# Gates and branch projections of the two mixers with the roles of weights and activations exchanged

## The chip, the cores and the metric

The kernel runs on one core of a Trainium2 chip. Its matrix products run on TensorE (PE in the profile, PEld for the loads of the stationary operand); VectorE (DVE), ScalarE (ACT) and GpSimd (POOL) do the elementwise work, and SyncE (SP) issues nearly all transfers of weights. The metric is the device time of one execution, in microseconds. The kernel before takes 1793.82 us (median of three runs, 1792.9 to 1797.88).

## What is computed

A trunk of two layers over 256 tokens of width 1024. Each layer is a mixer and then a feed-forward block (a dense SwiGLU in layer 0, a top-2-of-8 expert SwiGLU, the MoE, in layer 1), each followed by a residual LayerNorm with conditioning. The change touches the mixer only:

```
proj = h @ w_in       # conv_a, conv_b, q, k, v, ret_gate, gate_conv, gate_ret
u = causal_depthwise_conv(conv_a * sigmoid(conv_b), w_dw, b_dw)      # 31 taps
y_conv = silu(layer_norm(u)) @ w_conv_o                              # 1024 -> 1024
y_ret  = (silu(ret_gate) * head_norm(retention(q, k, v))) @ w_ret_o  # 2048 -> 1024
merged = sigmoid(gate_conv) * y_conv + sigmoid(gate_ret) * y_ret
mix    = merged @ w_out
```

## The kernel before

All weights are float32 in DRAM. They are streamed as units of 128 x 2048 (1 MB), and each unit is used in two pieces of 128 x 1024. A piece is split into a high and a low part: ACT rounds it to `wh` (L1657) and DVE subtracts to get `wl` (L1659). Activations are split likewise (`hH`/`hL`, `rH`/`rL`, `usH`/`usL`, `mH`/`mL`), and a product is the sum of three: high by high, high by low, low by high.

There are two forms of product. In `ws_block` the weights are stationary, 128 x 128 at a time, and the 256 tokens move: the result has channels on the partitions and tokens in a row. A piece takes 8 x 3 = 24 matmuls of 256 columns. In `ts_block` the activations of one tile of 128 tokens are stationary and 512 weight columns move: the result has tokens on the partitions. A piece takes 2 x 2 x 3 = 12 matmuls of 512 columns.

The order of the work is written by one list, `prog`, of units and of pieces of code, gone through in Python: before each piece the splits of the next pieces are emitted (`split_to`, `look` pieces ahead, with six `wh`/`wl` buffers), then what was put off by `defer(k, ...)` and has counted down, then the piece's own instructions. So every engine has a fixed order and an instruction that waits holds all that stands behind it on its engine. While the mixer's units run, the 31 taps of the convolution are done in portions by ACT and DVE (`run_bg`), and in layer 0 units of the conditioning (`adat`, by DVE) are woven in.

The stretch that the change touches is the last third of each mixer: 8 gate units (`F_unit`, gate_conv and gate_ret), 8 units of the retention branch's projection (`RO_unit`), 4 of the convolution branch's (`CO_unit`), then the output projection (`out_units`, already `ts_block`). All 20 use `ws_block` before: 40 pieces per layer. The tanh of a gate goes into `tg` by ACT (L738) after each unit; DVE multiplies it with the retention branch (L822, after each `RO_unit`), and after each `CO_unit` piece forms the merged sum `m` (L806, L807), which ACT and DVE split into `mH` and `mL` (L808, L809), with channels on the partitions as the output projection wants them. Inside the `RO` stage `conv_ln` normalises the convolution's result, turning it by transposes on PE (L766, L780). `end_tail` and `open_ln` close the mixer's buffers and open those of the LayerNorm.

Of the kernel before, what the change touches and what calls it, by code (L numbers as in the profile page):

```python
# [113 lines left out]
def _emit(tc, ctx, a):  # L114
# [3 lines left out]
    stream = ctx.enter_context(tc.tile_pool(name="stream", bufs=1))  # L118
    psum = ctx.enter_context(tc.tile_pool(name="psum", bufs=1, space=PSUM))
    small = ctx.enter_context(tc.tile_pool(name="small", bufs=4))  # L120
    ctx.enter_context(tc.manual_schedule())

    def bank(tag, bufs):
# [2 lines left out]
    def mm_bank():  # L126
        return bank("mm", 4)
# [4 lines left out]
    def sc_bank():  # L132
        return bank("sc", 2)
# [23 lines left out]
    def named(kind, u):  # L157
        u.kind = kind
        return u
# [154 lines left out]
    def defer(k, fn):  # L314
        deferred.append([k, fn])
# [126 lines left out]
    def mixer(l, raws, bound, fill=(), tail=()):  # L442
# [5 lines left out]
        def open_pool():  # L448
            S["mix"] = ExitStack()
            R["p"] = S["mix"].enter_context(tc.tile_pool(name=f"mixp{l}", bufs=1))  # L450
            S["head"] = ExitStack()
            R["hp"] = S["head"].enter_context(tc.tile_pool(name=f"headp{l}", bufs=1))
            R["upad"] = R["p"].tile([P, 8, 30 + T], F32, name="upad", tag="upad")
            if l:
                R["y"] = keep.tile([P, 8, T], F32, name="ycv", tag="z")
            R["rH"] = R["p"].tile([P, 16, T], F32R, name="rH")
# [267 lines left out]
        def end_heads():  # L724
            S["head"].close()
            S["tail"] = ExitStack()
            R["tp"] = S["tail"].enter_context(tc.tile_pool(name=f"tailp{l}", bufs=1))
            R["tg"] = R["tp"].tile([P, 8, 2, T], F32, name="tg")
            if l == 0:
                load_cb(keep, tag="gate")  # L730
            else:
                mixc["s"].close()
                state["px"] = ctx.enter_context(tc.tile_pool(name="extra", bufs=1, side="right"))
            for i, ps in R.pop("F_held", ()):
                F_drain(i, ps)

        def F_drain(i, ps):
            act.activation(R["tg"][:, i].rearrange("p s t -> p (s t)"), ps, AF.Tanh, scale=0.5)  # L738

        left = [18 + 2 * CL[l]]  # L740

# [1 line left out]
            left[0] -= 1  # L743
            return sum(c for c, _ in bg) / (left[0] + 1)

        def F_unit(i):
            def fn(s, w, wl):
                if s == 0:
                    R["F"] = mm_bank()
                ws_block(R["F"][:, s * T:(s + 1) * T], w, wl, state["hH"], state["hL"], 0, 8, True, True)  # L750
                run_bg(share())
                if s == 1 and "tg" in R:
                    F_drain(i, R["F"])
                elif s == 1:
                    R.setdefault("F_held", []).append((i, R["F"]))
            return named(f'F{l}', Unit(W["ws"][16 - W["w0"] + i], 2048, fn))

        def conv_ln():
            st = small.tile([P, 2, 2, 6], F32, name="cst", bufs=1)
            un = R["p"].tile([P, 2, D], F32, name="un", tag="upad")  # L760
            y = R["y"]
            for t in range(2):
                for hb in range(2):
                    ps = tp_bank() if hb else sc_bank()
                    for b in range(4):
                        pe.transpose(ps[:, b * P:(b + 1) * P], y[:, hb * 4 + b, tsl(t)], ident)  # L766
                    dve.bn_stats(st[:, t, hb, :], ps)
                    act.copy(un[:, t, hb * 512:hb * 512 + 512], ps)
            rs, nb = norm_scales(st, 2)
            for t in range(2):  # L770
                dve.tensor_scalar(un[:, t, :], un[:, t, :], rs[:, t:t + 1], nb[:, t:t + 1], op0=ALU.mult, op1=ALU.add)
            R["usH"] = keep.tile([P, 8, T], F32R, name="usH", tag="z")
            R["usL"] = R["tp"].tile([P, 8, T], F32R, name="usL", tag="usL")

            def back(q):
                ps = sc_bank()
                for i in range(2):
                    for t in range(2):
                        c = 2 * q + i
                        pe.transpose(ps[:, i * T + t * P:i * T + (t + 1) * P], un[:, t, c * P:(c + 1) * P], ident)  # L780
                for i in range(2):
                    c = 2 * q + i
                    us = R["tp"].tile([P, T], F32, name="us", tag="m", bufs=2)
                    act.activation(us, ps[:, i * T:(i + 1) * T], AF.Silu, bias=col("lc_b", l * 8 + c),
                                   scale=col("lc_g", l * 8 + c))
                    act.copy(R["usH"][:, c, :], us)
                    dve.tensor_tensor(R["usL"][:, c, :], us, R["usH"][:, c, :], op=ALU.subtract)
            for q in range(4):
                defer(BK[l] + q // 2, lambda q=q: back(q))

        early = 0 if l else 2
        units += [F_unit(i) for i in range(early)]
        units.append(end_heads)
        for i in range(early, 8):
            units.append(F_unit(i))

        def CO_unit(j):
            def fn(s, w, wl):
                i = 2 * j + s
                if i == 0:  # L800
# [9 lines left out]
            return Unit(W["ws"][24 - W["w0"] + j], 2048, fn)  # L810

        def RO_unit(i):
            def fn(s, w, wl):
                if s == 0:
                    R["RO"] = mm_bank()
# [4 lines left out]
                if s == 1:  # L820
                    tgr = R["tg"][:, i, 1, :]
                    dve.scalar_tensor_tensor(tgr, tgr, 1.0, ps, op0=ALU.add, op1=ALU.mult)  # L822
                    if i == CL[l]:
                        run_bg(1000)
                        defer(CD[l], conv_ln) if CD[l] else conv_ln()
                        if l == 0:
                            late["p"] = R["p"]
                            fetch_gbias(R["p"], 0, 0, tag="tap", bufs=2)
            return named(f'RO{l}', Unit(W["ro"][i], 2048, fn))

        for i in range(8):
            units.append(RO_unit(i))
# [235 lines left out]
    def moe():  # L1068
# [3 lines left out]
        def open_pools():  # L1072
# [9 lines left out]
            for nm, n, dt in (("ls", 8, F32), ("vals", 8, F32), ("idx", 8, U32), ("idf", 8, F32), ("msk", 8, F32),  # L1082
                              ("pos", 8, F32), ("comb", 8, F32)):
                R[nm] = p.tile([P, 2, n], dt, name=nm)
            R["E"] = p.tile([P, 2, 2, 8], F32, name="E")
            p.tile([P, 16], F32, name="pad0")
        opening.append(open_pools)

        def open_hg():
# [698 lines left out]
```

## Time and profile before

| | |
|---|---|
| median of the runs | 1793.82 us |
| profiled execution, its own time | 1797.46 us |
| its span, first to last instruction | 1795.7 us |
| mean granted TensorE clock | 0.982 of full speed |
| PE busy | 96% of the span |
| DVE busy / ACT busy / POOL busy | 88% / 65% / 14% |

A window of the trace shows the work and the waits of each engine in it; a busy PE is matmuls in flight, and since they overlap, the time that a stage takes is read from the starts of its first matmul and of the next stage's. The places in the execution: layer 0's gates from 238.7 us, its retention projection from 285.7, its convolution projection from 354.3, its output projection 380.0 to 402.0; layer 1's gates from 819.4, then 865.6, 914.3 and 937.3 to 959.2; the MoE from about 992 to the end.

### The profile page before, as it was taken

What the parts mean: (1) busy time and instruction counts of PE and PEld (TensorE: products, weight loads), DVE (VectorE), ACT (ScalarE), POOL (GpSimd) and SP (SyncE); (2) the same over time, 40 slices, a digit from 0 to 9 for tenths busy, and PEclk for the clock granted to TensorE, in tenths of its full rate; (3) what the DMA queues carried; (4) which work ended last, traced back from release to release, by engine and by line L of the source; (5) the groups of instructions that cost most, each with busy time, mean ns of one, the idle gap of its engine ahead of it and who ended that gap; (6) DMA issues with size and microseconds to landing.
All of it is one profiled execution on the core that took longest, in us unless ns stands there. A gap on an engine that the chain in (4) does not pass through costs nothing. (4 is left out here: it accounts for less than half of the span.)

```text
span 1795.7 us, 25962 instructions
## 1 busy us (share of the span) xinstructions
PE 1718.5 (96%) x9824; PEld 1481.6 (83%) x9824; DVE 1577.0 (88%) x2120; ACT 1162.8 (65%) x1644; POOL 248.5 (14%) x158
## 2 busy tenths in 40 slices
PE   6999899898999999999997999999999999999996
PEld 5978799787998698889995888888888888887785
DVE  8799879876778669999878999999999999998996
ACT  3566776634444365657643877778786878787773
POOL 5422302104000212210004100100002000100001
PEclk9999899999999999999998999999999999999998
DMA  9643445775779643445466789899998999898881
GB/s 363 248 164 144 161 176 213 291 283 216 299 291 356 231 188 141 177 173 191 165 269 250 313 328 365 324 351 388 357 368 315 384 357 373 309 374 327 326 339 64
DMA packets 71110, 491.72 MB, mean 274 GB/s; under 512 B 7953, under 2 KB 8721, under 8 KB 13634
## 3 DMA queue, kind: packets, MB, share of 16 engines
q1 hardware_dynamic: 69122, 484.28, 70.7%
q0 software_dynamic: 1568, 5.45, 0.9%
q8 instruction: 79, 1.29, 0.3%
q14 instruction: 53, 0.43, 0.1%
q10 hardware_dynamic: 288, 0.26, 0.0%
HBM read 488.92 MB, written 1.05 MB: 273 GB/s over the span
## 5 line engine op out<-in xcount | busy, mean ns | idle before, releaser
L1659 DVE TENSOR_TENSOR wl<-wf,wh 128x1024 fp32r<-128x1024 f32 (+1 forms) x813 | 999.3, 1255 | 96.9 <-ACT wh L1657 83.6
L1657 ACT CAST wh<-wf 128x1024 fp32r<-128x1024 f32 x819 | 839.1, 1048 | 151.0 <-PE ps_mm L136 87.1
L136 PE MATMUL ps_mm<-wh,hgH 128*128 128x512 f32 x704 | 283.4, 403 | 0.0
L136 PE MATMUL ps_mm<-wh,hgL 128*128 128x512 f32 x704 | 275.8, 392 | 0.0
L136 PE MATMUL ps_mm<-wl,hgH 128*128 128x512 f32 x704 | 274.3, 390 | 0.0
L136 PE MATMUL ps_mm<-hHn,wh 128*128 128x256 f32 x704 | 200.9, 285 | 0.5 <-ACT wh L1657 0.5
L136 PE MATMUL ps_mm<-hHn,wl 128*128 128x256 f32 x704 | 200.1, 284 | 0.8 <-DVE wl L1659 0.8
L136 PE MATMUL ps_mm<-hLn,wh 128*128 128x256 f32 x704 | 199.9, 284 | 0.0
L470 ACT ACTIVATE tap<-upad,cols 128x256 f32<-128x256 f32 x300 | 129.4, 500 | 93.8 <-DVE ycv L482 93.6
L136 PEld LDWEIGHTS ps_mm<-wh,hgL 128*128 128x128 f32 x704 | 132.1, 188 | 28.7
L136 PEld LDWEIGHTS ps_mm<-wl,hgH 128*128 128x128 f32 x704 | 132.6, 188 | 26.5 <-issue 1.0
L136 PEld LDWEIGHTS ps_mm<-wh,hgH 128*128 128x128 f32 x704 | 132.3, 188 | 25.7 <-issue 1.0
L136 PE MATMUL ps_mm<-wh,mb 128*128 128x512 f32 (+1 forms) x476 | 147.8, 384 | 0.0
L136 PEld LDWEIGHTS ps_mm<-hHn,wl 128*128 128x128 f32 x704 | 135.8, 193 | 1.2 <-DVE wl L1659 1.2
L136 PEld LDWEIGHTS ps_mm<-hHn,wh 128*128 128x128 f32 x704 | 135.8, 193 | 1.2 <-ACT wh L1657 0.7
L136 PEld LDWEIGHTS ps_mm<-hLn,wh 128*128 128x128 f32 x704 | 135.9, 193 | 0.4 <-issue 0.2
L482 DVE TENSOR_TENSOR ycv<-ycv,tap 128x1024 f32<-128x1024 f32 (+1 forms) x90 | 105.3, 1170 | 5.7 <-ACT tap L470 4.2
L136 PEld LDWEIGHTS ps_mm<-wh,mb 128*128 128x128 f32 x476 | 88.0, 188 | 19.2 <-issue 1.5
L488 DVE SCALAR_TENSOR_TENSOR ycv<-upad,cols,ycv 128x256 f32<-128x256 f32 x180 | 96.4, 572 | 0.6
L136 PE MATMUL ps_mm<-wl,mb 128*128 128x512 f32 (+1 forms) x238 | 90.8, 381 | 0.0
L1211 POOL CAST mb<-hT 128x512 fp32r<-128x512 f32 x12 | 10.4, 869 | 505.6 <-PE ps_sc L136 482.1
L263 DVE SCALAR_TENSOR_TENSOR wf<-wf,cb 128x1024 f32<-128x1024 f32 x58 | 76.1, 1348 | 0.9 <-DMA wf<-adat 0.9
(308 smaller groups left out, 3294.3 us busy)
## 6 DMA issues: line engine op xcount, KB each, us to landing
wf<-moe_gu SPq DMA_DIRECT2D x176, 1024.0 KB, 6.9
wf<-moe_d SPq DMA_DIRECT2D x75, 1024.0 KB, 6.4
wf<-ws SPq DMA_DIRECT2D x48, 1024.0 KB, 4.9
wf<-adat SPq DMA_DIRECT2D x32, 1024.0 KB, 5.9
wf<-ffn_gu SPq DMA_DIRECT2D x20, 1024.0 KB, 6.2
wf<-v SPq DMA_DIRECT2D x16, 1024.0 KB, 4.8
wf<-g SPq DMA_DIRECT2D x16, 1024.0 KB, 4.9
wf<-ro SPq DMA_DIRECT2D x16, 1024.0 KB, 4.8
```

What stands on the lines that cost most here:

```text
L136: pe.matmul(out, lhsT, rhs, start=start, stop=stop)
L263: dve.scalar_tensor_tensor(wj, wj, 1.0, state["cb"], op0=ALU.mult, op1=ALU.mult, accum_out=adac[:, l, c0:c0 + 1])
L470: act.activation(t[:, c - c0, :], u[:, c, j:j + T], AF.Copy, scale=taps[:, c, j:j + 1])
L482: dve.tensor_tensor(y, y, prod[j][:, 0:n, :], op=ALU.add)
L488: dve.scalar_tensor_tensor(y, u[:, c, j:j + T], taps[:, c, j:j + 1], y, op0=ALU.mult, op1=ALU.add)
L1211: pool.tensor_copy(R["tH"], h)
L1657: act.copy(w[:, 0:m], src)
L1659: eng.tensor_tensor(wl[:, 0:m], src, w[:, 0:m], op=ALU.subtract)
```

## The change

The 40 pieces per mixer go over to `ts_block`. Gate units are now a quarter of the 2048 gate columns by half of the depth (`q`, `half`), two units to a pair of banks, and the two tanh of a quarter come after its second unit. `RO` and `CO` are done by halves of 512 columns (`c`): four, respectively two, units to a half, each half in two banks, one for each tile of 128 tokens. The gating of the retention branch and the merged sum are done on 128 x 512 at the end of a half. The merged sum then has tokens on the partitions, and `m_split` turns it back with four transposes for each half and tile (16 per layer), put off by 2 pieces for the first tile and 3 for the second; its two splits read the transposes' bank. The first unit of the output projection now goes ahead of `end_tail` and `open_ln`. The weights are packed in DRAM to fit; bytes and transfers are the same in number. Four small paddings and one shared buffer in the MoE keep the layout of the memory.

```diff
+MS = (2, 3)
-            R["tg"] = R["tp"].tile([P, 8, 2, T], F32, name="tg")
+            R["tg"] = R["tp"].tile([P, 2, 4, 512], F32, name="tg")
...
+        def F_drain(q, banks):
+            for t in range(2):
+                act.activation(R["tg"][:, t, q, :], banks[t], AF.Tanh, scale=0.5)
...
-        def F_unit(i):
+        def F_unit(q, half):
             def fn(s, w, wl):
-                if s == 0:
-                    R["F"] = mm_bank()
-                ws_block(R["F"][:, s * T:(s + 1) * T], w, wl, state["hH"], state["hL"], 0, 8, True, True)
+                k0 = half * 4 + s * 2
+                if k0 == 0:
+                    R["F"] = [mm_bank(), mm_bank()]
+                for t in range(2):
+                    ts_block(R["F"][t], w, wl, state["hH"], state["hL"], k0, 2, tsl(t), k0 == 0, k0 == 6)
                 run_bg(share())
-                if s == 1 and "tg" in R:
-                    F_drain(i, R["F"])
+                if k0 == 6 and "tg" in R:
+                    F_drain(q, R["F"])
...
+        def m_split(c, t, m):
+            ps = sc_bank()
+            for b in range(4):
+                pe.transpose(ps[:, b * P:(b + 1) * P], m[:, b * P:(b + 1) * P], ident)
+            pv = ps.rearrange("p (b n) -> p b n", b=4)
+            hi, lo = R["mH"][:, 4 * c:4 * c + 4, tsl(t)], R["mL"][:, 4 * c:4 * c + 4, tsl(t)]
+            act.copy(hi, pv)
+            dve.tensor_tensor(lo, pv, hi, op=ALU.subtract)
 
         def CO_unit(j):
...
-                ps = mm_bank()[:, 0:T]
-                ws_block(ps, w, wl, R["usH"], R["usL"], 0, 8, True, True)
-                m = R["tp"].tile([P, T], F32, name="m", tag="m", bufs=2)
-                dve.scalar_tensor_tensor(m, R["tg"][:, i, 0, :], 1.0, ps, op0=ALU.add, op1=ALU.mult)
-                dve.tensor_tensor(m, m, R["tg"][:, i, 1, :], op=ALU.add)
-                act.copy(R["mH"][:, i, :], m)
-                dve.tensor_tensor(R["mL"][:, i, :], m, R["mH"][:, i, :], op=ALU.subtract)
+                if k == 0:
+                    R["CO"] = [mm_bank(), mm_bank()]
+                for t in range(2):
+                    ts_block(R["CO"][t], w, wl, R["usH"], R["usL"], k, 2, tsl(t), k == 0, k == 6)
+                if k < 6:
+                    return
+                for t in range(2):
+                    m = R["tp"].tile([P, 512], F32, name="m", tag="m", bufs=2)
+                    dve.scalar_tensor_tensor(m, R["tg"][:, t, c, :], 1.0, R["CO"][t], op0=ALU.add, op1=ALU.mult)
+                    dve.tensor_tensor(m, m, R["tg"][:, t, 2 + c, :], op=ALU.add)
+                    defer(MS[t], lambda t=t, m=m: m_split(c, t, m))
...
         def RO_unit(i):
...
-                ps = R["RO"][:, 0:T]
-                ws_block(ps, w, wl, R["rH"], R["rL"], s * 8, 8, s == 0, s == 1)
+                for t in range(2):
+                    ts_block(R["RO"][t], w, wl, R["rH"], R["rL"], k, 2, tsl(t), k == 0, k == 14)
...
+                if k == 14:
+                    for t in range(2):
+                        tgr = R["tg"][:, t, 2 + c, :]
+                        dve.scalar_tensor_tensor(tgr, tgr, 1.0, R["RO"][t], op0=ALU.add, op1=ALU.mult)
...
-        units.append(end_tail)
-        units.append(open_ln(l, 1, l, 3, 4, (l, 1)))
-        units.extend(tail)
         weave(units, raws, AFTER, SPARE)
-        prog.extend(out_units(W["out"], lambda: (R["mH"], R["mL"]), KD, 0.5, EARLY[2 * l]))
+        out = out_units(W["out"], lambda: (R["mH"], R["mL"]), KD, 0.5, EARLY[2 * l])
+        prog.extend(out[:1])
+        code(end_tail)
+        code(open_ln(l, 1, l, 3, 4, (l, 1)))
+        for f in tail:
+            code(f)
+        prog.extend(out[1:])
```

Order of ScalarE in layer 0's gate stage, before (`tap` is a tap of the convolution, `wh` a weight split, `tg` the tanh of a gate unit):

```order
L738 ACTIVATE tg<-ps_mm 128x512
L244 ACTIVATE cb<-cb 128x1024
L1657 CAST wh<-wf 128x1024
L470 ACTIVATE tap<-upad,cols 128x256 x4
L738 ACTIVATE tg<-ps_mm 128x512
L1657 CAST wh<-wf 128x1024
L470 ACTIVATE tap<-upad,cols 128x256 x4
L738 ACTIVATE tg<-ps_mm 128x512
L1657 CAST wh<-wf 128x1024 x2
```

The same place in the changed kernel:

```order
L742 ACTIVATE tg<-ps_mm 128x512 x2
L246 ACTIVATE cb<-cb 128x1024
L1685 CAST wh<-wf 128x1024
L473 ACTIVATE tap<-upad,cols 128x256 x4
L1685 CAST wh<-wf 128x1024
L473 ACTIVATE tap<-upad,cols 128x256 x4
L742 ACTIVATE tg<-ps_mm 128x512 x2
L1685 CAST wh<-wf 128x1024 x2
```

The tanh stand in pairs, with two pieces' worth of splits and taps more between one stop and the next.

Order of VectorE in layer 1 at the end of the convolution projection, before (`m` the merged sum, `mL` its low part, `gb` the first instructions of `open_ln`, `z` the residual behind the output projection):

```order
L1659 TENSOR_TENSOR wl<-wf,wh 128x1024
L806 SCALAR_TENSOR_TENSOR m<-tg,ps_mm 128x256
L807 TENSOR_TENSOR m<-m,tg 128x256
L809 TENSOR_TENSOR mL<-m,mH 128x256
L422 TENSOR_TENSOR gb<-cols,adac 128x8
L423 TENSOR_TENSOR gb<-cols,adac 128x8
L424 TENSOR_TENSOR gb<-gb,adac 128x8
L1659 TENSOR_TENSOR wl<-wf,wh 128x1024 x4
L395 SCALAR_TENSOR_TENSOR z<-ps_mm,gate 128x512
```

The same place in the changed kernel:

```order
L828 SCALAR_TENSOR_TENSOR m<-tg,ps_mm 128x512
L829 TENSOR_TENSOR m<-m,tg 128x512
L828 SCALAR_TENSOR_TENSOR m<-tg,ps_mm 128x512
L829 TENSOR_TENSOR m<-m,tg 128x512
L1687 TENSOR_TENSOR wl<-wf,wh 128x1024 x2
L810 TENSOR_TENSOR mL<-ps_sc,mH 128x4x128 x2
L424 TENSOR_TENSOR gb<-cols,adac 128x8
L425 TENSOR_TENSOR gb<-cols,adac 128x8
L426 TENSOR_TENSOR gb<-gb,adac 128x8
L1687 TENSOR_TENSOR wl<-wf,wh 128x1024 x2
L397 SCALAR_TENSOR_TENSOR z<-ps_mm,gate 128x512
```

The four instructions that came after every piece (the row group before stands there eight times) are gone; two sums of a half come together, and their low parts stand behind two splits.

Order of TensorE in the middle of layer 0's convolution projection, before (`wf` by `ca` is a unit of the conditioning):

```order
L136 MATMUL ps_mm<-usL,wh 128x256
L136 MATMUL ps_mm<-usH,wl 128x256
L285 MATMUL ps_tp<-wf,ca 32x512 x8
L136 MATMUL ps_mm<-usH,wh 128x256
L136 MATMUL ps_mm<-usL,wh 128x256
```

The same place in the changed kernel:

```order
L138 MATMUL ps_mm<-wh,usL 128x512
L287 MATMUL ps_tp<-wf,ca 32x512 x4
L806 MATMUL ps_sc<-ident,m 128x128 x4
L287 MATMUL ps_tp<-wf,ca 32x512 x4
L806 MATMUL ps_sc<-ident,m 128x128 x4
L138 MATMUL ps_mm<-wh,usH 128x512
```

The transposes of the first half's two tiles stand here directly behind that half, with one unit of the conditioning ahead of each, because those units count as pieces for `defer`.

## Rows read from the trace of the kernel before

**Rows 1.** The page's first part: busy time, share of the span, instructions.
```profile
PE 1718.5 (96%) x9824; PEld 1481.6 (83%) x9824; DVE 1577.0 (88%) x2120; ACT 1162.8 (65%) x1644; POOL 248.5 (14%) x158
```
**Rows 2.** Windows: stretch and length; busy of PE, PEld, DVE, ACT, POOL; clock; DMA.
```profile
816.52:865.56 49.04, 49.04 (x411) 49.04 (x410) 47.02 (x73) 35.95 (x62) 0.00 (x0) 1.00 0.49 178
865.56:888.18 22.62, 22.62 (x195) 22.62 (x193) 19.38 (x31) 12.69 (x19) 0.00 (x0) 1.00 0.51 181
914.29:937.33 23.04, 23.04 (x195) 23.04 (x194) 16.45 (x27) 8.15 (x12) 1.64 (x3) 1.00 0.85 342
```
**Rows 3.** Windows of layer 1 whose products already move 512 weight columns.
```profile
743.04:756.76 13.72, 13.72 (x62) 11.19 (x61) 13.69 (x20) 8.27 (x15) 6.47 (x4) 1.00 0.46 158
757.99:763.55 5.56, 5.56 (x27) 4.59 (x26) 5.53 (x10) 3.60 (x6) 0.00 (x0) 1.00 0.69 261
937.33:959.15 21.82, 21.82 (x98) 17.97 (x97) 17.89 (x36) 9.05 (x11) 2.33 (x3) 1.00 0.89 365
```
**Rows 4.** Windows: 16 transposes; nine gate pieces; three stretches of layer 0; the MoE.
```profile
888.18:889.84 1.66, 1.66 (x18) 1.66 (x17) 1.46 (x2) 0.00 (x0) 0.00 (x0) 1.00 0.21 79
828.96:852.72 23.76, 23.76 (x200) 23.76 (x199) 23.48 (x37) 19.56 (x33) 0.00 (x0) 1.00 0.60 220
238.74:285.68 46.94, 46.94 (x394) 46.93 (x393) 39.42 (x41) 39.72 (x72) 6.66 (x3) 1.00 0.56 201
285.68:337.63 51.95, 40.95 (x306) 39.72 (x305) 47.21 (x43) 30.43 (x54) 15.36 (x7) 0.88 0.68 250
354.34:380.03 25.69, 25.69 (x213) 23.64 (x212) 18.24 (x30) 12.19 (x18) 0.00 (x0) 1.00 0.70 274
...
990.00:1790.00 800.00, 788.67 (x3629) 645.27 (x3627) 747.13 (x864) 616.27 (x765) 38.65 (x33) 0.99 0.86 332
```
**Rows 5.** Waits of PE from 235 to 385 us: total, times, longest.
```profile
PE ps_tp L766 <- DVE ycv L482: 5.7, 1, 5.7
PE ps_mm L136 <- DVE wl L1659: 3.1, 3, 1.6
PE ps_mm L136 <- ACT wh L1657: 2.2, 1, 2.2
```
**Rows 6.** Waits of ACT for PE from 235 to 385 us: total, times, longest.
```profile
ACT tg L738 <- PE ps_mm L136: 5.9, 4, 2.6
```
**Rows 7.** Waits of DVE for PE in the same stretch.
```profile
DVE tg L822 <- PE ps_mm L136: 2.2, 2, 1.4
```
**Rows 8.** ScalarE in order of time in layer 0's gates: start, duration, wait before.
```profile
274.36 0.60 ACT L738 ACTIVATE tg<-ps_mm 128x512 f32<-128x512 f32 x1 [2.62 <-PE ps_mm L136]
```
**Rows 9.** DVE by line and shape, 800 to 970 us: busy, mean ns.
```profile
L822 DVE SCALAR_TENSOR_TENSOR tg<-tg,ps_mm 128x256 f32<-128x256 f32 x8 | 3.3, 418 | 5.0 <-PE ps_mm L136 5.0
...
L395 DVE SCALAR_TENSOR_TENSOR z<-ps_mm,gate 128x512 f32<-128x512 f32 x4 | 2.8, 688 | 1.7 <-PE ps_mm L136 1.7
...
L582 DVE TENSOR_TENSOR rL<-ps_tp,rH 128x512 fp32r<-128x512 f32 x2 | 1.3, 683 | 0.0
```
**Rows 10.** VectorE in order of time round the end of layer 1's convolution projection.
```profile
936.88 1.23 DVE L1659 TENSOR_TENSOR wl<-wf,wh 128x1024 fp32r<-128x1024 f32 x1 [0.53 <-ACT wh L1657]
938.02 0.41 DVE L806 SCALAR_TENSOR_TENSOR m<-tg,ps_mm 128x256 f32<-128x256 f32 x1
938.47 0.42 DVE L807 TENSOR_TENSOR m<-m,tg 128x256 f32<-128x256 f32 x1
939.37 0.43 DVE L809 TENSOR_TENSOR mL<-m,mH 128x256 fp32r<-128x256 f32 x1 [0.47 <-ACT mH L808]
940.32 1.22 DVE L1659 TENSOR_TENSOR wl<-wf,wh 128x1024 fp32r<-128x1024 f32 x1 [0.53 <-ACT wh L1657]
941.46 0.41 DVE L806 SCALAR_TENSOR_TENSOR m<-tg,ps_mm 128x256 f32<-128x256 f32 x1
```
**Rows 11.** The transfers of the conditioning behind layer 0's mixer, as SP issues them.
```profile
386.66 2.02 SPq L1642 DMA_DIRECT2D wf<-ada  x4
```
**Rows 12.** VectorE where layer 1's residual begins, behind the output projection.
```profile
959.35 0.69 DVE L395 SCALAR_TENSOR_TENSOR z<-ps_mm,gate 128x512 f32<-128x512 f32 x1 [1.02 <-PE ps_mm L136]
```

More of the change, by code (lines that the diff above doesn't have):

```diff
@@ L120, in _emit @@
     small = ctx.enter_context(tc.tile_pool(name="small", bufs=4))
+    small.tile([P, 32], F32, name="padl", bufs=1)
     ctx.enter_context(tc.manual_schedule())
@@ L455, in open_pool @@
                 R["y"] = keep.tile([P, 8, T], F32, name="ycv", tag="z")
+            R["p"].tile([P, 16], F32, name="padr")
             R["rH"] = R["p"].tile([P, 16, T], F32R, name="rH")
@@ L733, in end_heads @@
                 state["px"] = ctx.enter_context(tc.tile_pool(name="extra", bufs=1, side="right"))
[L734 to L738, printed above, removed]
+            for q, banks in R.pop("F_held", ()):
+                F_drain(q, banks)
+        def F_drain(q, banks):
+            for t in range(2):
+                act.activation(R["tg"][:, t, q, :], banks[t], AF.Tanh, scale=0.5)
         left = [18 + 2 * CL[l]]
@@ L782, in back @@
                     c = 2 * q + i
-                    us = R["tp"].tile([P, T], F32, name="us", tag="m", bufs=2)
+                    us = R["tp"].tile([P, 512], F32, name="us", tag="m", bufs=2)[:, 0:T]
                     act.activation(us, ps[:, i * T:(i + 1) * T], AF.Silu, bias=col("lc_b", l * 8 + c),
@@ L789, in conv_ln @@
                 defer(BK[l] + q // 2, lambda q=q: back(q))
+        gates = [F_unit(q, half) for q in range(4) for half in range(2)]
         early = 0 if l else 2
-        units += [F_unit(i) for i in range(early)]
+        units += gates[:early]
         units.append(end_heads)
-        for i in range(early, 8):
-            units.append(F_unit(i))
+        units += gates[early:]
+        def m_split(c, t, m):
[6 more added lines that the diff above has]
+            dve.tensor_tensor(lo, pv, hi, op=ALU.subtract)
@@ L797, in CO_unit @@
         def CO_unit(j):
+            c, f = divmod(j, 2)
             def fn(s, w, wl):
-                i = 2 * j + s
-                if i == 0:
+                k = f * 4 + s * 2
+                if j == 0 and s == 0:
                     R["mH"] = keep.tile([P, 8, T], F32R, name="mH", tag="hH")
                     R["mL"] = keep.tile([P, 8, T], F32R, name="mL", tag="hL")
-                ps = mm_bank()[:, 0:T]
-                ws_block(ps, w, wl, R["usH"], R["usL"], 0, 8, True, True)
-                m = R["tp"].tile([P, T], F32, name="m", tag="m", bufs=2)
@@ L819, in fn @@
                     run_bg(share())
[L820 to L828, printed above, removed]
@@ L829, in RO_unit @@
-            return named(f'RO{l}', Unit(W["ro"][i], 2048, fn))
+                if k == 14:
+                    for t in range(2):
+                        tgr = R["tg"][:, t, 2 + c, :]
+                        dve.scalar_tensor_tensor(tgr, tgr, 1.0, R["RO"][t], op0=ALU.add, op1=ALU.mult)
+                if s == 1 and i == CL[l]:
+                    run_bg(1000)
+                    defer(CD[l], conv_ln) if CD[l] else conv_ln()
+                    if l == 0:
+                        late["p"] = R["p"]
+                        fetch_gbias(R["p"], 0, 0, tag="tap", bufs=2)
@@ L1081, in open_pools @@
             state["hgx"] = p
-            for nm, n, dt in (("ls", 8, F32), ("vals", 8, F32), ("idx", 8, U32), ("idf", 8, F32), ("msk", 8, F32),
+            for nm, n, dt in (("ls", 8, F32), ("vals", 8, F32), ("idx", 8, U32), ("msk", 8, F32),
                               ("pos", 8, F32), ("comb", 8, F32)):
@@ L1085, in open_pools @@
             R["E"] = p.tile([P, 2, 2, 8], F32, name="E")
-            p.tile([P, 16], F32, name="pad0")
+            R["idf"] = R["ls"]
         opening.append(open_pools)
@@ L1737 @@
             ws.append(_pack_ws([blk(3072, 2 * h), blk(3072, 2 * h + 1)]))
-        ws += [_pack_ws([blk(8192, i), blk(9216, i)]) for i in range(8)]
-        co = w_conv_o[l]
-        ws += [_pack_ws([co[:, 2 * j * P:(2 * j + 1) * P], co[:, (2 * j + 1) * P:(2 * j + 2) * P]]) for j in range(4)]
         arrays[f"ws{l}"] = np.stack(ws)
@@ L1747 @@
                                               for f in range(2)]) for h in range(H)])
-        arrays[f"ro{l}"] = np.stack([_pack_ws([w_ret_o[l][:, i * P:(i + 1) * P]]) for i in range(8)])
+        arrays[f"f{l}"] = np.stack([np.stack([_pack_ts(w[f * 512:(f + 1) * 512, 8192 + q * 512:8704 + q * 512])
+                                              for f in range(2)]) for q in range(4)])
+        for nm, v, n in (("ro", w_ret_o[l], 4), ("co", w_conv_o[l], 2)):
+            arrays[f"{nm}{l}"] = np.stack([np.stack([_pack_ts(v[f * 512:(f + 1) * 512, c * 512:(c + 1) * 512])
+                                                     for f in range(n)]) for c in range(2)])
         arrays[f"out{l}"] = np.stack([np.stack([_pack_ts(w_out[l][f * 512:(f + 1) * 512, q * 512:(q + 1) * 512])
```

16 lines of the change are left out of this document (10 added, 6 removed).

## Prediction

> **What bounds the kernel now.** I read the busy shares first, then a table of windows over the stretches that the change touches, then the waits, and at last single instructions. The page has PE busy for 96% of the span [rows 1], which says little by itself, because overlapped matmuls count as busy; so I take the time of a stage from start to start. In layer 1 the gates, the retention projection and the convolution projection show PE busy for the whole of every window at full clock [rows 2]: there is no wait to remove, only work to shorten. DVE is close behind: 47.0 of 49.0 us in the gates. In layer 0 the gates are the same picture (46.94 of 46.94 us), but from 285.7 to 337.6 us PE is busy for only 40.95 of 51.95 us, DVE for 47.21, and the granted clock is down to 0.88 [rows 4]. PE's waits there end with DVE and ACT: 5.7 us once for the convolution's sum, 3.1 us for `wl`, 2.2 us for `wh` [rows 5]. That stretch belongs to DVE. From 354.3 us layer 0 is PE's again (25.69 of 25.69), and so is the MoE (788.7 of 800 us): what is won ahead of it is not swallowed by transfers there [rows 4].
>
> **The price of a piece.** The window of layer 1's gates holds 17 pieces of 24 matmuls in 49.04 us, 2.885 us each; the retention projection 8 in 22.62, 2.83; the convolution projection 8 in 23.04, 2.88 [rows 2]. (The counts in the rows are a few higher, by matmuls that lap over the edges.) The new form already runs in this kernel: five pieces of 12 matmuls in 13.72 us, 2.744 each; two in 5.56, 2.78; eight of the output projection in 21.82, 2.73 [rows 3]. I take 2.744, since that window is in the same mixer with DVE just as full (13.69 of 13.72). The columns streamed are the same (24 x 256 = 12 x 512), so what is saved is what each matmul costs beyond its columns: 0.14 us for a gate piece, 0.083 for a retention piece, 0.136 for a convolution piece. Per layer 16 x 0.14 + 16 x 0.083 + 8 x 0.136 = 2.25 + 1.35 + 1.1 = 4.7 us of PE time.
>
> **What is added on PE.** 16 transposes of 128 x 128 per layer. Sixteen transposes of that size took 1.66 us [rows 4]: 0.104 each, 1.66 us per layer.
>
> **Layer 1** is PE's throughout, so it gives 4.7 - 1.66 = 3.0 us, if DVE keeps up. Nine gate pieces of DVE's work (window 828.96 to 852.72, from one `wl` to that nine pieces later) took 23.76 us, 2.64 a piece, with DVE busy 23.48 of it [rows 4]: less than 2.744, by 0.1. The pace holds, with little to spare. In the retention stage DVE also loses the gating after each unit (8 x 418 ns becomes 4 of 512 columns, for which the nearest row, a product out of a bank of that width, has 688 ns [rows 9]): 3.3 us become 2.75. Bounds: 0 if DVE is the next limit at once, 3.0 as worked out, and 3.7 if the 2.73 us of the output projection's pieces are reached (40 x 0.0165 more).
>
> **Layer 0.** PE's gain in the gates counts only if DVE's stretch behind them also starts earlier. It does, I think: ACT stops for PE at the tanh of a unit, 5.9 us in four waits [rows 6], the longest 2.62 us at 274.36 [rows 8], and DVE stands behind ACT's splits. In the new order ACT stops after every second unit only; the stop at 274.36 stays one, since it falls at the end of the third quarter, behind 12 gate pieces: 12 x 0.14 = 1.7 us earlier. From there on DVE has its own work to the end of the convolution; up to that point it loses six gatings of 418 ns and gets two of 688: 1.1 us less. Its waits for PE at these gatings, 2.2 us in two, the longer one 1.4 [rows 7], become rarer, since there is one stop in eight pieces instead of four; I take 0.4 of 0 to 1.4. Behind that stretch PE leads again: 4 x 0.083 + 8 x 0.136 - 1.66 = 0.2 us lost. Sum 1.7 + 1.1 + 0.4 - 0.2 = 3.0 us, with bounds of -0.2 (nothing passes DVE's stretch) and 4.0.
>
> **Handing the merged sum over.** This is the wait that the change adds: PE's transposes wait for `m`, and behind them in PE's order stand the output projection's pieces; those of the second half (from the third piece on) wait for `mH` and `mL`. Before, DVE was late here: the last `m` starts at 941.46, 4.1 us after PE had gone on at 937.33, because each piece cost DVE a round of 3.44 us (938.02 to 941.46) through ACT and back, against PE's 2.88 [rows 10]. That harmed nobody, since the piece that wanted it came late. In the new order the rounds are gone: for a half DVE has four `wl` of 1.22, four operations of 0.69 and two of 0.68 [rows 9, 10], 9.0 us, against 4 x 2.744 + 0.83 for the transposes, 11.8 us of PE. So DVE is idle when the half ends. The first tile's matmuls of the last piece end half a piece, 1.37 us, ahead of the second's, so its `m` is ready some 0.1 us after the half's end. The transposes ask for it 2.74 us after the end, behind a piece of the output projection, and in the middle of layer 0 after about 0.9 us, behind one unit of the conditioning. The second tile's `m` follows 1.4 us later and is asked for one piece (in layer 0's middle, one unit) later. `mL` stands behind two `wl` and ends at about 4.7 us; its piece starts at 6.3. I cost the wait at 0, hidden by that first unit; the cover is 1.6 us thick at its thinnest.
>
> **The rest.** `open_ln` behind the first output unit moves POOL's loads and, in layer 0, four transfers of the conditioning. Before, these left at 386.66 [rows 11], 6.6 us after the output projection began, held by the last `mL`; now the last reader of that memory is the last transpose, at about 6.3 us after its beginning: no later, cost 0. If they came late, each microsecond would stand ahead of the LayerNorm; they have 15 us until 402. Behind layer 1's output projection DVE waits for PE (1.02 us [rows 12]), so the residual starts as much earlier as PE ends. Transfers, splits and the taps are the same in number; paddings cost nothing.
>
> **Sum.** 3.0 + 3.0 = 6.0 us. The profiled execution took 1797.46 us (span 1795.7 and 1.8 around it), 3.6 above the median of the runs, and would come to 1791.5; from the median, 1793.82 - 6.0 = 1787.8 us. About 0.3%, 5.4 us, is what a measurement of this kernel can tell from no change (1788.4 and 1799.2 are the marks), and the forecast lies hardly beyond it.
>
> **Rivals.** *DVE keeps layer 0's gain.* For it: PE's waits in that stretch [rows 5] grow by whatever PE wins before; against it: ACT's stops for PE in the gates. Layer 0 then loses its 0.2: 1793.8 - 3.0 + 0.2 = 1791.0 us.
>
> *The merged sum comes late, and the kernel is slower.* If DVE is as late at a half's end as before, 4.1 us [rows 10], the first tile's `m` is ready 1.4 us behind that. PE then idles 4.1 + 1.4 - 2.74 = 2.8 us at each layer's end and 4.1 + 1.4 - 0.9 = 4.6 in the middle of layer 0: 10.2 us, and the time is 1798.0. It decides against the change from a lateness L with 3L - 2.2 = 6.0, L = 2.7 us; longer operations could put it at 1800. Against it speaks that DVE's round through ACT, which made the lateness, is gone.
>
> *The new form is not cheaper here.* By the dearest of the rows, 2.78 [rows 3], against the cheapest old piece, 2.83 [rows 2], a piece saves 0.045: 80 x 0.045 = 3.6 us, less 3.3 for the transposes: 1793.5 us. Against it: that window has attention scores beside it. The Trainium skill has a rule that leads here ("TensorE: Matmul & The Clock Gate", section "Back-to-back issue gap"): a warm matmul costs its columns at 2.4 GHz and 2.5 ns more. By that, estimated, 24 x 109.2 ns = 2.62 us stand against 12 x 215.8 = 2.59, a gain of 2.4 us over 80 pieces, and with the transposes the kernel would be 0.9 slower, at 1794.7. The trace does not agree: a piece is 2.83 to 2.885 us in the one form and 2.744 in the other, so a matmul costs about 11 to 15 ns beyond its columns here.
>
> *More than that.* ACT stops half as often in the gates and DVE is no longer late at the output projection; if DVE's stretch in layer 0 starts 2 to 3 us earlier still (the waits of 5.9 us in [rows 6] are what there is), the time is 1785.
>
> **Chances.** Forecast (1786 to 1790) 0.47; DVE keeps layer 0's gain 0.20; late sum 0.15; not cheaper 0.07; more 0.11. Beyond 1788.4 lie 0.7 of the forecast and all of the last: faster 0.44. Above 1799.2 lies half of the late sum: slower 0.08. The rest, 0.48, is no change. The range of 1784.5 to 1796 leaves out the worse part of the late sum and a little on the other side; the forecast's own is 1786 to 1790.
>
> **What would show it.** In the new profile the gates and both projections of layer 1 should take 2.74 us a piece with PE busy throughout, and the stretch from the first gate (816.52 + 2.885) to the output projection (937.33) 117.9 - 3.0 = 114.9 us. In layer 0 the stop for the tanh nearest 274 should lie 1.7 us earlier and the convolution's sum some 3 us earlier. PE should show no wait of over 0.5 us for `m` or `mL`. Waits of PE for `m` of several microseconds would make the prediction wrong, and so would gate pieces in which PE waits for `wl`, DVE's 2.64 us being too near.

## The result and the profile after

The changed kernel took 1785.97 us (median of six runs, 1781.4 to 1787.1) against 1796.74 for six runs of before, to which the three of the opening belong: a ratio of 0.9936, 95% interval 0.9917 to 0.9954, some 11 us. The forecast was 6.0 us less, 1787.8. The direction was right and the size half of what came; the time lies within the range of 1784.5 to 1796 and just outside the forecast's own 1786 to 1790. In the trace the span fell from 1795.7 to 1784.6 us.

The page's first part of the kernel after:
```profile
PE 1706.6 (96%) x8896; PEld 1435.7 (80%) x8896; DVE 1570.2 (88%) x2088; ACT 1161.6 (65%) x1636; POOL 250.1 (14%) x158
```
Windows of the kernel after, columns as in [rows 2]: layer 1's gates, eight retention pieces, convolution and output projection; then layer 0's gates, its stretch up to the end of the convolution's sum and its transposes, its convolution projection:
```profile
817.53:861.08 43.55, 43.55 (x195) 36.05 (x193) 42.16 (x66) 31.60 (x55) 0.00 (x0) 1.00 0.52 182
861.08:882.84 21.76, 21.76 (x97) 17.97 (x96) 20.98 (x32) 13.93 (x22) 0.00 (x0) 1.00 0.52 181
908.18:930.90 22.72, 22.72 (x106) 18.80 (x104) 16.57 (x19) 9.45 (x11) 1.64 (x3) 1.00 1.01 395
930.90:953.61 22.71, 22.71 (x106) 18.77 (x105) 16.38 (x33) 7.56 (x9) 2.34 (x3) 1.00 0.76 308
238.20:282.65 44.45, 44.45 (x201) 36.87 (x201) 38.66 (x41) 39.45 (x72) 5.88 (x3) 1.00 0.60 206
282.65:332.19 49.54, 38.93 (x161) 31.23 (x160) 47.33 (x40) 30.88 (x56) 16.54 (x7) 0.89 0.74 267
349.21:375.08 25.87, 25.87 (x124) 19.44 (x122) 19.23 (x23) 13.30 (x16) 0.00 (x0) 1.00 0.78 287
```
Against [rows 2, 4]: 16 gate pieces in 43.55 us are 2.72 each, a retention piece is 2.72 too, PE busy in every window of layer 1, DVE 42.16 of 43.55. Of these windows only layer 0's middle stretch still has PE idle.

PE's waits of the kernel after, 235 to 385 us, against [rows 5] (total, times, longest):
```profile
PE ps_tp L772 <- DVE ycv L485: 5.4, 1, 5.4
PE ps_mm L138 <- ACT wh L1685: 3.0, 1, 3.0
PE ps_mm L138 <- DVE wl L1687: 2.2, 2, 1.1
```
ACT's waits for PE at the gates in the same stretch, against [rows 6]:
```profile
ACT tg L742 <- PE ps_mm L138: 3.4, 2, 2.6
```
ScalarE's stop for a tanh and what follows it, against [rows 8]; the last row is the kernel before, behind the tanh of [rows 8]:
```profile
270.61 0.60 ACT L742 ACTIVATE tg<-ps_mm 128x512 f32<-128x512 f32 x1 [2.64 <-PE ps_mm L138]
271.97 0.60 ACT L742 ACTIVATE tg<-ps_mm 128x512 f32<-128x512 f32 x1 [0.76 <-PE ps_mm L138]
272.47 1.99 ACT L1685 CAST wh<-wf 128x1024 fp32r<-128x1024 f32 x2
```
```profile
274.85 1.99 ACT L1657 CAST wh<-wf 128x1024 fp32r<-128x1024 f32 x2
```
ACT has two waits instead of four, and both belong to one pair of tanh. The first of the pair runs 3.75 us earlier than the long stop's tanh before, but its bank holds one tile of tokens and is done half a piece ahead of the other's. What DVE depends on is when ACT goes on to its splits: at 272.47 us instead of 274.85, 2.4 earlier, and 0.5 of that the gates had at their first product already (238.24 against 238.74). PE's wait for the convolution's sum is nearly as long as before (5.4 against 5.7), and the sum's transposes end 5.4 us earlier, at 332.19 instead of 337.63.

PE's row of time at the handover in layer 1, after: the sum's transposes behind the first unit of the output projection's products:
```profile
933.39 0.39 PE L138 MATMUL ps_mm<-wh,mL 128*128 128x512 f32 x1
933.62 0.60 PE L806 MATMUL ps_sc<-ident,m 128*128 128x128 f32 x4
933.97 0.48 PE L138 MATMUL ps_mm<-wh,mH 128*128 128x512 f32 x1
```
No row there has a wait in brackets: the handover costs only its transposes.

The surprise lies behind the mixers, where no instruction is changed. The experts' stage, first gate product to last operation, before and then after:
```profile
992.57:1779.28 786.71, 786.10 (x3614) 642.94 (x3612) 737.83 (x839) 611.65 (x757) 34.29 (x30) 1.00 0.88 337
```
```profile
988.02:1768.50 780.48, 779.87 (x3614) 642.35 (x3612) 736.12 (x839) 611.64 (x757) 35.08 (x30) 1.00 0.89 339
```
The same 3614 products on PE, none of them waiting in either kernel to speak of, the same clock, and 6.2 us less. And the feed-forward's down projection in layer 0, also unchanged, is longer: 63.97 us instead of 61.44 to the start of its last product. PE now waits for weights there, which it does not in the trace of before (waits after, 539 to 610 us):
```profile
PE ps_mm L138 <- DVE wl L1687: 1.7, 3, 0.8
PE ps_mm L138 <- ACT wh L1685: 1.1, 1, 1.1
```

By stages, the 11.1 us of the trace are 3.6 in each mixer from its first gate product on and 6.2 in the experts, less 2.5 in the down projection and 1.0 between layer 1's output projection and the experts (34.4 us instead of 33.4; the other kernels lie between 33.1 and 34.3). Another 1.2 us are spread over the rest of the execution.

### The profile page after: what moved, and what is told of

Read it like the earlier page. It is cut to its first block, busy times and chain, and to the rows that moved or that the text cites. A ratio compares the mean times of both kernels' runs of the same rounds, so it can differ in the third digit from the quotient of the medians.

```text
span 1784.6 us, 24061 instructions
## 1 busy us (share of the span) xinstructions
PE 1706.6 (96%) x8896; PEld 1435.7 (80%) x8896; DVE 1570.2 (88%) x2088; ACT 1161.6 (65%) x1636; POOL 250.1 (14%) x158
## 5 line engine op out<-in xcount | busy, mean ns | idle before, releaser
L138 PE MATMUL ps_mm<-hHn,wh 128*128 128x256 f32 x576 | 164.6, 286 | 0.5 <-ACT wh L1685 0.5
L138 PE MATMUL ps_mm<-hHn,wl 128*128 128x256 f32 x576 | 163.8, 284 | 0.8 <-DVE wl L1687 0.8
L138 PE MATMUL ps_mm<-hLn,wh 128*128 128x256 f32 x576 | 163.6, 284 | 0.0
L138 PEld LDWEIGHTS ps_mm<-hHn,wh 128*128 128x128 f32 x576 | 111.2, 193 | 1.2 <-ACT wh L1685 0.7
L138 PEld LDWEIGHTS ps_mm<-hHn,wl 128*128 128x128 f32 x576 | 111.2, 193 | 1.0 <-DVE wl L1687 1.0
L138 PEld LDWEIGHTS ps_mm<-hLn,wh 128*128 128x128 f32 x576 | 111.3, 193 | 0.4 <-issue 0.2
L138 PE MATMUL ps_mm<-wh,hHn 128*128 128x512 f32 x208 | 84.6, 407 | 0.0
L138 PE MATMUL ps_mm<-wh,hLn 128*128 128x512 f32 x208 | 81.3, 391 | 1.7 <-POOL hLn L393 1.7
```

The source lines that it names most:

```text
L138: pe.matmul(out, lhsT, rhs, start=start, stop=stop)
```

## The experiments

Two theories stood at first: the experts' gain comes from where the buffers lie (A), or from chance, the stream or the weights' places in DRAM (B).

**Buffers alone** (`layout_only`): of the change only this.
```
+    small.tile([P, 32], F32, name="padl", bufs=1)
+            R["p"].tile([P, 16], F32, name="padr")
-... ("idf", 8, F32) ...; p.tile([P, 16], F32, name="pad0")
+            R["idf"] = R["ls"]
```


> The kernel before with nothing changed but where its buffers lie: the 128 and 64 bytes of padding, the index tile laid over the scores tile and the old pad left out, as in the change. All products as before. Theory A (the experts' stage, 6.5 us shorter in the trace of the change although its instructions are the same, is shorter because its buffers moved): 4.5 to 6.5 us faster than before, some 1791, with two gate/up units of the experts at 5.69 us instead of 5.71. Theory B (the experts' stage differs from execution to execution, or through the weights' places in DRAM or the shorter stream of instructions): within 2 us of before, the experts' stage about 800 us long as before.

Measured 1790.67 us, ratio 0.9969 (0.9958 to 0.9981). The experts' stage:
```profile
990.46:1770.80 780.34, 779.73 (x3614) 642.33 (x3612) 736.01 (x839) 611.62 (x757) 34.76 (x30) 1.00 0.88 340
```
Theory A holds: half of the change's gain is there without any of its products. The opening's "four small paddings and one shared buffer" that "keep the layout of the memory" are these lines: two paddings come in, one goes, the index tile shares a buffer, and together they move the layout.

**Products alone** (`no_pads`): the change with those four lines undone.

> The change with all its products, but its buffers as before: no padding of 128 and 64 bytes, the index tile and the old pad back. Theory A: the experts' stage goes back to its old length, 5 to 6.5 us slower than the change, some 1791.5, the mixers' gain kept. Theory B: as the change, 1786 within 2 us.

Measured 1793.78 us, ratio 0.9987 (0.9978 to 0.9995): slower than A said, since the new products suffer as well (below). The experts' stage has its old length:
```profile
989.42:1776.14 786.72, 786.11 (x3614) 642.89 (x3612) 737.95 (x839) 611.73 (x757) 34.59 (x30) 1.00 0.89 337
```

**Which move matters** (`pad128_all`: before with `padl` alone; `pad64`: the change with `[P, 16]` for `padl`'s `[P, 32]`).

> The kernel before with the 128 bytes of padding alone, the index tile and the old pad as they were: all that lies above it moves by 128 bytes, the experts' input with it, which the change leaves where it was. Theory 'same offset' (a product is fast where its activations lie at the same offset, modulo 256 bytes, as the converted weights): the down projections of the experts, whose activations come to that offset, fall from 219 to 214.5 ns a product as in the change, and the gate and up products, whose activations leave it, rise from 228 to 230 ns or more. Theory 'any move' (the old place clashed with another buffer): both fall. Theory 'tile of the index' (the aliasing did it): nothing falls.

> The change with 64 bytes of padding in place of 128, so that the activations of the experts and of the retention's projection lie 64 bytes off the converted weights' offset modulo 128 or 256. Theory 'same offset': the experts' down projections go back to some 219 ns a product, the gate and up products rise from 227.5 to 229 or more, and the experts' stage is 6 us or more longer than the change's 780. Theory 'any move': they stay at 214.5 ns and the stage at 780 us.

One run each, with no interval: 1790.63 and 1790.55 us. The experts' stage of the one, then of the other:
```profile
988.17:1772.63 784.46, 783.85 (x3614) 642.47 (x3612) 737.70 (x839) 612.05 (x758) 34.30 (x30) 1.00 0.88 338
```
```profile
990.64:1772.57 781.93, 781.32 (x3614) 642.30 (x3612) 737.54 (x839) 612.05 (x758) 34.98 (x30) 1.00 0.89 339
```
Two things in these expectations were wrong. The 214.5 and 219 ns mixed products of 256 and 512 columns; for 512 alone the figures are 227.7 and 232.3. And the experts' input stayed at the same address in every kernel here, so whether the gate and up products would rise was not tried. What was tried fits "same offset". The mean spacing of one 512-column product to the next, worked out from the timelines, by how far the activations (stationary) lie from the converted weights (moving), modulo 256 bytes by the kernels' memory maps:
```
ns from start to start        same   -64    -128   +64
experts' down (ma)            227.7  229.0  232.3
feed-forward's down (a)       227.1  228.9  232.6
retention projection (r)      227.3  229.1         233.4
convolution projection (us)*  227.4  231.1         230.9
  same: after; -64: pad64; -128, +64: no_pads.  * only its low half moves; the high half is always at "same"
```
The experts have a second pair of buffers (`mb`) for these activations, which `pad128_all` left at -128 while `ma` came to "same", and `pad64` the other way round with `ma` at -64. Within one execution each follows its own place: `ma` 227.7 and `mb` 232.7 ns in `pad128_all`, 229.0 and 227.4 in `pad64`; both stages lie between 780.4 and 786.7. Of the 1122 down products 990 have 512 columns; at 4.9 ns each they give 4.8 us (those of 256 columns take 119.7 to 119.9 ns in both kernels). The 2112 gate and up products at 227.6 instead of 228.2 ns give 1.3, though neither their activations nor the weights' buffers moved. Together that is 6.1 of the 6.2.

`pad128_all` shows something else. Its retention projection has the old form, 256 columns with weights stationary, and lies at -64. Eight pieces of it in layer 1:
```profile
863.34:885.12 21.78, 21.78 (x195) 21.78 (x194) 19.36 (x31) 12.73 (x19) 0.00 (x0) 1.00 0.50 174
```
That is 2.72 us a piece, as little as in the changed kernel. For this stage a move of 128 bytes alone does what the new form does.

**Length or role** (`halves`): what makes a piece cheaper.
```
-  ts_block(...)   one product of 512 columns
+  ts_half(...)    for h in range(2): the same on columns h*256 to h*256+256
```


> The change with each product of its gates and both branch projections in two instructions of 256 weight columns instead of one of 512, activations stationary as in the change: 24 products and 24 loads for a piece, as many as before with the roles swapped. Theory 'length' (half as many instructions for the same columns is what made a piece 2.72 us instead of 2.88): pieces back at 2.85 to 2.9 us, 5 to 7 us in each mixer, the whole 7 to 12 us slower than the change. Theory 'role' (weights as the moving operand, or their place, made it cheaper): pieces stay at 2.72, within 1.5 us of the change.

Measured 1791.11 us, ratio 0.9968 (0.9957 to 0.998). Its gates, eight retention pieces and convolution projection in layer 1:
```profile
816.36:862.44 46.08, 46.08 (x386) 46.08 (x385) 44.65 (x70) 33.01 (x57) 0.00 (x0) 1.00 0.51 183
862.44:884.50 22.06, 22.06 (x186) 22.06 (x185) 18.06 (x28) 12.78 (x19) 0.00 (x0) 1.00 0.52 192
911.98:935.88 23.90, 23.90 (x202) 23.90 (x201) 16.52 (x18) 9.36 (x10) 1.64 (x3) 1.00 1.00 398
```
Gates at 2.88 us a piece, to the hundredth the 46.08 that before takes for its 16, and the whole is where the moved buffers alone put it. So, at the same offset, it is the length of the instruction, not the swapped roles. The whole is 5.1 us slower than the change, less than the 7 to 12 expected: the mixers are longer by 6.2 and 3.5 us in the trace, the down projection shorter by 3.5. Not separated is the product from its weight load, since each product here has one of its own; PEld is busy for the whole 46.08 us of these gates and for 36.05 of the change's 43.55. Stage by stage, in us from a stage's first product to the next stage's, for the output and down projections to the start of their last product:
```
                              before  layout_only  halves   after   no_pads  pad128_all
layer 1: gates                 46.08     46.09      46.08   43.55    43.55     46.08
  retention, convolution's LN  48.73     49.55      49.54   47.10    48.33     47.18
  convolution projection       23.04     23.04      23.90   22.72    23.04     22.62
  output projection            21.59     21.56      22.52   22.48    22.48     21.58
layer 0's output ends at      401.67    399.68     399.98  397.57   396.35    401.00
feed-forward's down            61.44     60.73      60.52   63.97    65.05     60.25
experts                       786.71    780.34     780.45  780.48   786.72    784.46
```
In `halves`, `after` and `no_pads` the convolution projection and the output projection hold eight transposes of the merged sum each.

**Transposes twice** (`twice`): the four `pe.transpose` of `m_split` repeated.

> The change with the 16 transposes of each mixer's merged sum done twice over. If they cost what the 16 before the convolution's normalisation show (1.66 us), the stretch from the convolution's first product to the output projection's last is 1.6 to 1.8 us longer in each layer, 48.4 to 50.1 and 45.2 to 46.9. If a wait for the sum hides them, it is as long as in the change.

One run, 1784.64 us. From the convolution's first product to the output projection's last: 50.07 us instead of 48.36 in layer 0, 46.89 instead of 45.20 in layer 1: 1.7 each, as expected. A single run whose whole was not slower cannot show 3.4 us: executions of one kernel differ by more, and its down projection took 62.1 us, the change's 64.0.

**Handover without cover** (`handover`): `end_tail`, `open_ln` and the rest of the tail ahead of all output units.

> The change with the transposes of the merged sum's second half placed right behind the convolution's last products, ahead of every unit of the output projection, so that nothing covers the two VectorE operations on each of the two token tiles. My theory (the output projection's first unit hides them): each mixer gets a wait of TensorE for m of 1.4 to 3.4 us in front of these transposes, and the whole is 3 to 7 us slower than the change. The rival (the sum is ready by then anyhow, or the following stage takes the wait up): within 1 us of the change.

Measured 1785.61 us, ratio 0.994 (0.9927 to 0.9953): no slower than the change's 0.9936, so the 3 to 7 us of my theory did not come. PE's wait at layer 1's handover in that kernel:
```profile
930.95 0.63 PE L806 MATMUL ps_sc<-ident,m 128*128 128x128 f32 x4 [0.24 <-DVE m L829]
932.31 0.63 PE L806 MATMUL ps_sc<-ident,m 128*128 128x128 f32 x4 [0.73 <-DVE m L829]
```
DVE's first operation on the sum there:
```profile
929.39 0.69 DVE L828 SCALAR_TENSOR_TENSOR m<-tg,ps_mm 128x512 f32<-128x512 f32 x1 [1.32 <-PE ps_mm L138]
```
Bare, the handover waits 1.0 us in a layer (the same in layer 0), below the 1.4 to 3.4 expected: DVE stands idle for 1.3 us ahead of the first `m`, so it is not late. The same stretches grow by 1.3 us each (49.66, 46.51); at the end that is not seen, and the two intervals could not tell 2.6 us.

**One layer at a time** (`layer1_only`, `layer0_only`: buffers as in the change, the other layer's gates and projections as before).

> The change in layer 1's mixer alone; layer 0's gates and branch projections with weights stationary, as before. From the traces of both kernels layer 1's mixer gives 3.7 us and layer 0's 3.6 (of which 2.5 are lost again in the feed-forward's down projection), the experts' stage 6.5. Theory A: the buffers lie as in the change, so 1796.7 - 3.7 - 6.5 = some 1786.5, the down projection back at 61.8 us. Theory B, with the experts' 6.5 us tied to the products or to chance: 1790 to 1793.

> The change in layer 0's mixer alone, buffers placed as in the change; layer 1's gates and branch projections with weights stationary, as before. Layer 0's output projection should end 2 to 4 us earlier than with the buffers moved alone. Theory 'taken back' (the feed-forward's down projection in layer 0 ends when its weights and layer 1's modulation weights, both moved in that stretch, have landed, at 603 to 604 us of the span whether it begins at 539 or at 543): within 1 us of the kernel with the buffers moved alone, some 1790.5. Theory 'kept' (what layer 0's mixer saves lasts to the end): 3 to 4 us less than that, some 1787.

Measured 1787.25 us (0.9951; 0.9939 to 0.9964) and 1787.94 us (0.9956; 0.9942 to 0.997). Layer 1 alone came near theory A's 1786.5. Layer 0 alone kept its gain: in the traces the output ends 1.74 us ahead of `layout_only` and the kernel 1.4, by the medians the kernel is 2.7 us faster. That is more than "taken back" allows and less than "kept" said. Its down projection, without much wait:
```profile
540.65:601.86 61.21, 60.51 (x265) 49.16 (x264) 46.80 (x70) 23.73 (x25) 0.53 (x1) 1.00 0.81 315
```
The six kernels with the new layer 0 and this queue took 61.2 to 68.0 us there (mean 64.1), the five with 256-column products in layer 0 60.3 to 62.4 (61.1), though its instructions are the same and there is one trace of each.

**The loads beside the down projection** (`spread`, then `rest2` and `rest0`): layer 1's 16 modulation loads; in the change 12 stand among the 20 gate and up units and 4 among the down units. `spread` has 10 and 6 (its expectation speaks of loads behind the last gate and up unit; there are none), `rest2` 14 and 2, `rest0` 16 and 0.
```
-NREST = 4        +NREST = 6, behind down units 0, 1, 3, 4, 6, 7    (spread)
-NREST = 4        +NREST = 2                                        (rest2; 0 in rest0)
-rate = min(1.0, ...)   +rate = min(1.6, ...)   lets two loads follow one unit (rest2, rest0)
```


> The change with the loads and reductions of layer 1's modulation weights spread evenly: none is added behind the last gate and up unit of the feed-forward, and six stand behind the first, second, fourth, fifth, seventh and eighth unit of its down projection, where two and four stood behind each other. Theory 'taken back' (two MB for each 5.6 us are asked for in the down projection's first half, and its weights come late): the down projection, 64.0 us in the change, takes 60 to 61, TensorE waits for no weights in it, and the whole is 2 to 3.5 us faster than the change, some 1783. If the down projection's length is not set by these loads: 62 to 65 us as in the change, 1786.

> The change with two of layer 1's modulation weight loads moved from the feed-forward's down projection to its gate and up units: 14 spread over the 20 gate and up units and 2 behind the first two down units, where 12 and 4 stood. Theory 'slots' (each such load among the down units takes one of the four weight buffers and VectorE's time just where the down projection's weights are wanted; six of them made it 70.5 us long, four 64.0): the down projection takes 60.5 to 62 us and the whole 1783 to 1784. Theory 'moved' (the gate and up stretch waits instead): that stretch is 2 us or more longer and the whole 1786 or more.

> The change with all 16 of these loads spread over the 20 gate and up units and none in the down projection. Theory 'slots': the down projection runs without a wait, 60 to 60.5 us, the gate and up stretch (119 us of products) as long as before within 1 us, the whole 1782.5 to 1783.5. Theory 'moved': the gate and up units wait for their own weights, 2 us or more, and the gain is gone, 1785 to 1788.

Measured 1789.11 (0.996; 0.9946 to 0.9974), 1782.81 (0.9931; 0.9918 to 0.9945) and 1785.37 us (0.9942; 0.9929 to 0.9955). The window of the down projection in `spread`, and PE's waits there:
```profile
539.03:609.55 70.52, 64.15 (x266) 49.82 (x264) 49.26 (x75) 22.43 (x24) 0.53 (x1) 0.98 0.81 298
```
```profile
PE ps_mm L138 <- DVE wl L1687: 6.3, 6, 2.2
```
The same window in `rest2`, and in `rest0`:
```profile
539.96:600.72 60.76, 60.28 (x265) 49.21 (x264) 42.64 (x63) 23.85 (x25) 0.53 (x1) 1.00 0.76 284
```
```profile
549.92:609.56 59.64, 59.64 (x265) 49.37 (x264) 37.31 (x53) 23.95 (x25) 0.53 (x1) 1.00 0.66 244
```
A wait of PE for its weights in the gate and up units of `rest0`, in the order of time:
```profile
540.70 0.58 PE L138 MATMUL ps_mm<-hHn,wh 128*128 128x256 f32 x1 [2.40 <-ACT wh L1685]
```
`spread` fell and turned the theory round: not how evenly the loads lie but how many stand among the down units goes with the wait. Six make 70.5 us, four 64.0, two 60.8, none 59.6. With none the gate and up stretch pays: 145.3 us instead of 136.4. These are one trace each, four made 61.2 to 68.0 in the kernels above, and the traces of `spread` and `rest0` are the slowest of their runs (1792.26 and 1790.86 us), so that their other runs may wait less. By the runs only `rest2` against `spread` is clear of the intervals; `rest2` is the fastest by its median, but its interval overlaps the change's.

## Why the prediction was right or wrong

- **The price of a piece** was right as a mechanism, a little small: 2.72 us where 2.744 was taken. `halves` shows the cause named, what an instruction (a product with its weight load) costs beyond its columns: two products of 256 columns take 240.0 ns, one of 512 takes 226.8, in gates whose operands lie alike. What the prediction did not have is that this price depends on where the operands lie, by up to 6.5 ns a product. The rival "not cheaper" is refuted for the gates. The 2.5 ns that the Trainium skill gives ("TensorE: Matmul & The Clock Gate", "Back-to-back issue gap"), there for an isolated matmul, do not hold here: 227.3 ns for 512 columns are 14 beyond 213.3 at 2.4 GHz.
- **Layer 1**, forecast 3.0: its four stages sum to 139.4 us before and 135.85 after, 3.6 less; from the first gate to the output projection 113.4 us, where 114.9 was said. Against the moved buffers alone (140.2) it is 4.4, since these made the old retention form 0.8 dearer. DVE kept up.
- **The transposes** at 1.66 us a layer: 1.7 by doubling them.
- **Layer 0**, forecast 3.0: from its first gate product to the start of the output projection's last one the seven kernels with the new layer 0 and its handover as changed take 159.4 us on average, the four with the old 162.5: 3.1. (By the output's end alone it is 397.0 against 401.0 us, but 0.8 of that is there before the first gate.) Two terms were off against each other. The sum's transposes come 4.0 us earlier counted from the first gate, where 3.2 was said; behind them TensorE loses 0.9, where 0.2 was said. ACT goes on behind the tanh 1.9 us earlier counted likewise, as forecast (1.7). The rival "DVE keeps layer 0's gain" did not come.
- **The handover** at 0: right, and safer than I made it. The lateness L, which had to reach 2.7 us, is none: DVE waits for PE ahead of the first `m`, and with the cover gone PE's whole wait is 1.0 us a layer.
- **"The rest"** is the step that failed, in "paddings cost nothing" and in costing the unchanged stages at nothing. Moving the buffers is worth 0.31% by itself (0.19 to 0.42), some 5.6 us and about half of the result; 6.2 us of the trace are the experts' stage. Against that, the down projection behind layer 0 lost 2.5 us that I had not looked for.
- So the sum of 6.0 came near what the products give with the buffers alike (`layout_only` to the change: 4.7 us by the medians, 5.9 by the ratios, uncertain by some 4), and the time came out lower because of a term at zero. That it still lies in the range is in part luck: a gain and a loss that were both left out. It is nearest to the rival "more than that" (1785), whose mechanism did not come: ACT went on 1.9 us earlier, not 2 to 3 more than the forecast's 1.7. The opening's median of three runs, 1793.82, was also 2.9 us below that of six.

Open: why the down projection, with the same queue, takes 60 us in one kernel and 68 in another, beyond that it is shortest with few loads beside it; what made the experts' gate and up products 0.6 ns faster; and whether the price beyond the columns is the product's or its weight load's.

## What to carry to other kernels

Before costing a pad or a renamed tile at nothing, work out which operands of later stages it moves against each other: here moves of 64 and 128 bytes were worth about as much as rewriting 80 pieces of products. Where TensorE is busy throughout, fewer and longer matmuls pay an amount for each one saved (here 13 ns, with the operands at the same offset), which the trace's spacing gives directly. What is won ahead of a stage with transfers of its own can be lost there, so try the loads beside that stage again after the change.

## What was unexpected of the hardware

- A 512-column product took 227.0 to 227.7 ns with its stationary activations at the same offset modulo 256 bytes as the moving weights, 229 at 64 bytes below, 232 to 233 at 128 below, 233.4 at 64 above (retention), 231 in the convolution projection, where only the low half had moved. The granted clock was 1.00 in the experts' stage and in layer 1's mixer.
- For 256-column products with weights stationary the best place was another one: in layer 1's retention projection, at a granted clock of 1.00, 113.7 ns at -64 (`pad128_all`), 117.8 at +64 (before), 119.9 at the same offset (`layout_only`). Why was not tried.
